# Two layers of a hybrid encoder: GLA values loaded a group earlier, other shares of dense work, the decays moved, the convolutions' gate product on another engine

## The chip, the cores and the metric

The kernel runs on one core of a Trainium2 chip. The metric is the device time of one execution in microseconds (us), the median of the runs shown. The engines of the core work side by side, each through its own list of instructions in order: TensorE (PE, with its weight loads as PEld), VectorE (DVE), ScalarE (ACT), GpSimd (POOL) and SyncE (SP), which here issues the transfers between the core's memory and the chip's main memory.

## What is computed

Two layers, each with one input projection whose columns feed three mixers: gated linear attention (GLA), a gated delta rule with short convolutions, and cross-attention into 256 memory tokens. Sequence 1024, model width 1024, all in f32.

```python
def _layer(x, mem, ...):
    h = _rmsnorm(x, norm_w)
    proj = jnp.einsum('btd,de->bte', h, w_in)
    (gla_q, gla_k, gla_v, gla_z, gla_lr, gdn_qkv, gdn_z, gdn_b, gdn_a, xa_q, xa_z) = _split_cols(proj, IN_SIZES)
    ...
    o1 = _run_bidir(_gla_chunked, (q1, k1, v1, log_alpha_fwd), (q1, k1, v1, log_alpha_bwd))
    o1 = _rmsnorm(o1, gla_norm_w) * silu(gla_z)
    qkv = jax.nn.silu(_centred_depthwise_conv(gdn_qkv, gdn_conv_w))      # 5 taps
    q2, k2, v2 = _split_cols(qkv, ...)
    q2 = _l2norm(q2) * (GDN_DK ** -0.5)
    k2 = _l2norm(k2)
    ...
    o2 = _run_bidir(_gated_delta_chunked, (q2, k2, v2, g_fwd, beta_fwd), (q2, k2, v2, g_bwd, beta_bwd))
    o2 = _rmsnorm(o2, gdn_norm_w) * silu(gdn_z)
    o3 = softmax-attention of xa_q into the memory tokens, normed, * silu(xa_z)
    return x + concat(o1, o2, o3) @ w_out

def _gla_chunked(q, k, v, g):       # per chunk: cumulated gates, a state update from k and v, then
    ...                             # S_t = dec * S_{t-1} + st
def _gated_delta_chunked(q, k, v, g, beta):
    diff = gc[..., :, None] - gc[..., None, :]
    decay = jnp.where(incl, jnp.exp(jnp.where(incl, diff, 0.0)), 0.0)
    ...
```

## The kernel before

**Dense work.** The input projection is cut into tiles of 128 columns by 1024 tokens. `dense_gen` is a generator that walks over them; one step of it is a unit of six matmuls (weights and activations are split into a high and a low half, Hh and Hl against wh and wl). `pull` takes units worth a number of nanoseconds, `upto` takes them until a tile is done. The other phases run beside this generator and pull units between their own steps, so that TensorE has something to do. At a tile's second half `conv_sink` or `spill` takes it on.

**Convolutions (`conv_sink`, `phase_proj`).** Nine tiles feed the convolutions, k first, then v, then q. ScalarE copies a tile out of PSUM into `pad` and, scaled by the middle tap, into `acc`. VectorE adds the four other taps (four `scalar_tensor_tensor`, L537). ScalarE forms the sigmoid in three passes (`pad`), and the product `acc * pad` ends the SiLU. TensorE transposes it to token order (`conv_t`), k and q are normed (`l2norm`) and transposed back (`back_t`).

**Decays (`decays`).** For each of four heads: a subtract on POOL (N minus gB, pinned in its place), a minimum with a cap on VectorE, an exponential on ScalarE. One `next(dec)` emits one head. The kernel before emits heads in the k loop and, what is left, in the v loop.

**The chain (`phase_mix`, `chain`).** The gated delta rule goes through 16 steps of both directions, one chunk each; `chain_load` brings kq, row, kv and qkt for a step. Between the pieces of a step `filler` emits other work by a time budget: the GLA gates and states, then dense units, then the mixing tiles (`mixes`: memory attention xa and GLA output), then the output projection.

**GLA (`gla_pre`).** Eight groups (a pair of heads, a direction, a half of the sequence). `gate` loads q and k, forms the gates and stores the scaled pair ge_d; `state` loads the values gv, transposes, and forms the states, which it stores (s_d). Gates run two groups ahead of states. gv has one buffer before. The order of the work is that of the code, with a scheduler that reorders within each engine; all loads and stores stand in SyncE's one queue.

**Constants that spread the dense units.** `DEN0` units after the second piece of the GLA work, `PRE_D` units spread over its 24 pieces, `MIX0` units between the last state and the first mixing tile, `MIXN` the pace after that. `DC0` is the index of the k loop from which decays are emitted.

## Time and profile before

| what | value |
| --- | --- |
| median of 3 runs | 1389.29 us (1388.51 to 1390.2) |
| the profiled execution | 1388.65 us, span 1386.9 us |
| PE busy | 1214.1 us (88% of the span) |
| DVE, ACT, POOL busy | 827.7, 614.0, 462.4 us |
| chain that ended last | PE 48%, DVE 15%, DMA 14%, POOL 6%, SPq 6%, ACT 6%, issue 5% |
| PE idle before mm matmuls | 22.2 us, of it 17.5 until the accumulator on ACT |
| POOL products acc*pad | 18 instructions, 45.5 us |

How to read it: the span is the time between the first and the last instruction of the profiled execution. Busy time is the sum of an engine's instructions; weight loads (PEld) overlap the matmuls. Work that a wait holds up stands in brackets behind an instruction, with the idle time before it and the name of what ended it. Lines such as L537 are lines of the kernel before; the new kernel's lines are one or two lower in the first half of the file. A row's "x8" is a count of instructions.

### The profile page before, as it was taken

The numbers are of one execution on the slowest core, as the hardware profiler recorded it, in microseconds if no ns is written. First come the engines' busy times: TensorE is split into PE (matmuls) and PEld (weight loads), VectorE is DVE, ScalarE is ACT, GpSimd is POOL, SyncE is SP. The second block draws the span as 40 slices with busy tenths as digits, with TensorE's granted clock in tenths as the row PEclk, the third lists the DMA queues.
The fourth block names the chain that finished last, engine by engine and source line by source line (L and its number), as shares of the span: only waits on it lengthen the run. The fifth ranks groups of instructions, "written<-read, shape, count | busy, mean of one in ns | idle before, by whom it ended". The sixth has DMA issues, their size and how long they took to land.

```text
span 1386.9 us, 25327 instructions
## 1 busy us (share of the span) xinstructions
PE 1214.1 (88%) x9962; PEld 991.1 (71%) x9962; DVE 827.7 (60%) x1255; ACT 614.0 (44%) x1293; POOL 462.4 (33%) x493
## 2 busy tenths in 40 slices
PE   6998799998888647999989987999977887589997
PEld 6986588776666546787879866887756666468886
DVE  5336855795376655655373568647944786465553
ACT  5334655343556432233163356543345565232432
POOL 4026442294335231211230444423943443220111
PEclk9999999999999868999999998999999898699999
DMA  7151234532999895345471513345228999853532
GB/s 230 57 129 46 86 112 130 190 99 70 206 234 240 252 243 116 92 134 154 155 226 48 135 31 118 88 133 186 91 86 220 241 250 251 220 158 95 160 104 107
DMA packets 299319, 205.38 MB, mean 148 GB/s; under 512 B 144064, under 2 KB 267392, under 8 KB 299200
## 3 DMA queue, kind: packets, MB, share of 16 engines
q1 hardware_dynamic: 297040, 195.89, 51.5%
q10 hardware_dynamic: 2016, 7.34, 1.6%
q8 instruction: 79, 1.29, 0.4%
q0 software_dynamic: 144, 0.52, 0.1%
q14 instruction: 40, 0.33, 0.1%
HBM read 145.11 MB, written 58.59 MB: 147 GB/s over the span
## 4 chain that ended last, share of the span: by engine, by line
PE 48%; DVE 15%; DMA 14%; POOL 6%; SPq 6%; ACT 6%; issue 5%; DVEq 0%; ACTq 0%; POOLq 0%
PE mm L98 31%; DVE acc L537 6%; PE cp L98 4%; PE x L98 3%; PE tr L101 3%; DMA gv<-vg 3%; PE R L98 2%; POOL X L90 2%; DMA wor<-in_w_out_dram 2%; POOL tmp L90 2%; PE gb L98 1%; DMA ge_d<-qe 1%; ACT pad L84 1%; DMA wr<-in_w_in_dram 1%; POOL sp L90 1%
## 5 line engine op out<-in xcount | busy, mean ns | idle before, releaser
L98 PE MATMUL mm<-Hh,wh 128*128 128x512 f32 x736 | 311.1, 423 | 22.2 <-ACT acc L84 17.5
L98 PE MATMUL mm<-Hl,wh 128*128 128x512 f32 x736 | 295.9, 402 | 0.0
L98 PE MATMUL mm<-Hh,wl 128*128 128x512 f32 x736 | 295.5, 402 | 0.0
L90 POOL TENSOR_TENSOR wl<-wr,wh 128x1024 fp32r<-128x1024 f32 x46 | 119.4, 2596 | 277.0 <-ACT wh L84 250.3
L98 PEld LDWEIGHTS mm<-Hh,wh 128*128 128x128 f32 x736 | 143.3, 195 | 59.8 <-ACT acc L84 20.9
L537 DVE SCALAR_TENSOR_TENSOR acc<-pad,convw,acc 128x1024 f32<-128x1024 f32 x72 | 141.4, 1963 | 67.5 <-ACT acc L84 53.1
L98 PE MATMUL mm<-wo,oh 128*128 128x512 f32 x512 | 166.7, 407 | 0.3 <-DVE xr L87 0.3
L98 PEld LDWEIGHTS mm<-Hh,wl 128*128 128x128 f32 x736 | 143.2, 195 | 32.3
L98 PEld LDWEIGHTS mm<-Hl,wh 128*128 128x128 f32 x736 | 144.1, 196 | 26.2
L90 POOL TENSOR_TENSOR ol<-z,oh 128x512 fp32r<-128x512 f32 x32 | 41.0, 1286 | 197.9 <-ACT oh L84 196.8
L98 PEld LDWEIGHTS mm<-wo,oh 128*128 128x128 f32 x512 | 90.5, 189 | 18.6 <-issue 0.9
L98 PE MATMUL mm<-wo,ol 128*128 128x512 f32 x256 | 101.2, 395 | 0.0
L90 POOL TENSOR_TENSOR acc<-acc,pad 128x1024 f32<-128x1024 f32 x18 | 45.5, 2528 | 109.8 <-ACT pad L84 109.8
L84 ACT ACTIVATE wh<-wr 128x1024 fp32r<-128x1024 f32 x46 | 48.5, 1054 | 68.6 <-PE mm L98 57.6
L90 POOL TENSOR_TENSOR kq<-kq,row 96x512 f32<-96x512 f32 x30 | 41.8, 1395 | 101.6 <-DMA kq<-kq_d 45.7
L90 POOL TENSOR_TENSOR S<-S,dec 96x384 f32<-96x384 f32 x56 | 53.3, 967 | 62.5 <-DVE S L87 53.8
L90 POOL TENSOR_TENSOR sp<-sp,sg 128x512 f32<-128x512 f32 x32 | 45.9, 1434 | 59.7 <-ACT sg L84 41.8
L84 ACT ACTIVATE oh<-z 128x512 fp32r<-128x512 f32 x32 | 20.2, 632 | 85.0 <-DVE z L87 84.9
L98 PE MATMUL cp<-S,kq 96*64 96x96 f32 x960 | 51.7, 256 | 7.0 <-DVE oa L87 2.4
L98 PEld LDWEIGHTS mm<-wo,ol 128*128 128x128 f32 x256 | 48.1, 188 | 11.5
L98 PEld LDWEIGHTS cp<-S,kq 96*64 96x64 f32 x960 | 44.2, 141 | 16.0 <-issue 7.0
L87 DVE TENSOR_TENSOR xr<-mm,xr 128x512 f32<-128x512 f32 x32 | 22.1, 690 | 50.7 <-PE mm L98 24.7
(294 smaller groups left out, 2439.5 us busy)
## 6 DMA issues: line engine op xcount, KB each, us to landing
wr<-in_w_in_dram SPq DMA_DIRECT2D x46, 512.0 KB, 3.9
kq<-kq_d SPq DMA_DIRECT2D x64, 192.0 KB, 4.5
kv<-kv_d SPq DMA_DIRECT2D x64, 192.0 KB, 4.4
zT<-sp SPq DMA_DIRECT2D x32, 256.0 KB, 3.4
ge_d<-qe SPq DMA_DIRECT2D x32, 256.0 KB, 4.4
wor<-in_w_out_dram SPq DMA_DIRECT2D x16, 512.0 KB, 5.4
z<-zT SPq DMA_DIRECT2D x16, 512.0 KB, 4.4
gqk<-ge_d SPq DMA_DIRECT2D x16, 512.0 KB, 4.2
```

What stands on the lines that cost most here:

```text
L84: return self.nc.scalar.activation(out, in_, func, **kw)
L87: return self.nc.vector.tensor_tensor(out, a, b, op=op)
L90: return self.nc.gpsimd.tensor_tensor(out, a, b, op=op)
L98: return self.pin(self.nc.tensor.matmul(*args, **kw))
L101: return self.pin(self.nc.tensor.transpose(*args, **kw))
L537: nc.vector.scalar_tensor_tensor(acc, pad[:, j:j + T], self.convw[:, f, j:j + 1], acc, op0=ALU.mult, op1=ALU.add)
```

## The change

The new kernel has four edits. (1) The product that ends a convolution's SiLU is on VectorE (`tt`) where it was on POOL (`ptt`): 18 instructions. (2) The decays' heads are emitted in the q loop, from its second convolution on, the rest before q's norm; the `next(dec)` of the k and v loops and `DC0` are gone. (3) The load of a GLA group's values is in a function of its own, `values`, called once ahead of everything and then one group before its state; the values have two buffers. (4) `PRE_D` 32 to 24, `MIX0` 5 to 8, `DEN0` 6 to 4.

```diff
-PRE_D = 32
+PRE_D = 24
-DC0 = 0
-MIX0 = 5
+MIX0 = 8
-DEN0 = 6
+DEN0 = 4
...
                 self.sigmoid(pad[:, 0:T], acc)
-                self.ptt(acc, acc, pad[:, 0:T], ALU.mult)
+                self.tt(acc, acc, pad[:, 0:T], ALU.mult)
                 self.conv_out[f] = acc
...
             self.conv_t(3 + i, k_tok[:, :, i * 128:i * 128 + 128])
-            if i >= DC0:
-                next(dec, None)
         self.l2norm(ST, k_tok, 1.0)
...
             v_out(1 + i)
-            next(dec, None)
...
             self.conv_t(i, q_tok[:, :, i * 128:i * 128 + 128])
+            if i:
+                next(dec, None)
         for _ in dec:
             pass
         self.l2norm(ST, q_tok, HD ** -0.5)
...
+        def values(pr, d, hf):
+            v = G.tile([P, 4, 2, HD], F32, tag="gv", name="gv", bufs=2)
+            nc.sync.dma_start(v.rearrange("p t a b -> p t (a b)"),
+                              self.vg[hf * 4:hf * 4 + 4, :, pr * 192:pr * 192 + 192].rearrange("t p c -> p t c"))
+            st["v"] = st.get("v", []) + [v]
+
         def state(pr, d, hf):
...
-            v = G.tile([P, 4, 2, HD], F32, tag="gv", name="gv", bufs=1)
-            nc.sync.dma_start(v.rearrange("p t a b -> p t (a b)"),
-                              self.vg[hf * 4:hf * 4 + 4, :, pr * 192:pr * 192 + 192].rearrange("t p c -> p t c"))
+            v = st["v"].pop(0)
...
+        values(*groups[0])
         for g in groups[0:2]:
             gate(*g)
             yield
         for i, g in enumerate(groups):
             if i + 2 < len(groups):
                 gate(*groups[i + 2])
                 yield
+            if i + 1 < len(groups):
+                values(*groups[i + 1])
             for _ in state(*g):
                 yield
             yield
```

What this does to the order of instructions, in layer 0. First SyncE, in the middle of the GLA groups. ge_d is the store of a gate's result, qkin the loads of a gate's q and k, gv the values, s_d the store of a state; kq, row, kv and qkt belong to the chain, wor is a raw piece of the output weights. The kernel before:

```order
L1174 DMA ge_d<-qe 64x2x512 x2
L1142 DMA qkin<-qg 128x512
L1143 DMA qkin<-kg 128x512
L993 DMA kq<-kq_d 96x8x64 x2
L1192 DMA gv<-vg 128x4x192
L995 DMA row<-row_d 96x4x64 x2
L1425 DMA wor<-in_w_out_dram 128x2x512
L1222 DMA s_d<-sb 64x4x96 x2
L997 DMA kv<-kv_d 64x2x384
L998 DMA qkt<-qkd 64x4x64
```

The same place in the new kernel:

```order
L1172 DMA ge_d<-qe 64x2x512 x2
L1140 DMA qkin<-qg 128x512
L1141 DMA qkin<-kg 128x512
L993 DMA row<-row_d 96x4x64
L991 DMA kq<-kq_d 96x8x64
L1186 DMA gv<-vg 128x4x192
L991 DMA kq<-kq_d 96x8x64
L993 DMA row<-row_d 96x4x64
L1224 DMA s_d<-sb 64x4x96 x2
L995 DMA kv<-kv_d 64x2x384 x2
L996 DMA qkt<-qkd 64x4x64 x2
```

The place of gv in the list is alike, but before it brings the values of the state that s_d stores a few rows below, and now those of the next group's state.

Next VectorE at the first convolutions. acc is a convolution's accumulator, tok the k values in token order, N the decays, cap their cap. The kernel before:

```order
L537 SCALAR_TENSOR_TENSOR acc<-pad,convw,acc 128x1024 x8
L87 TENSOR_TENSOR N<-N,cap 128x1024
L115 COPY tok<-tr 128x4x128
L537 SCALAR_TENSOR_TENSOR acc<-pad,convw,acc 128x1024 x4
L87 TENSOR_TENSOR N<-N,cap 128x1024
```

The new kernel:

```order
L536 SCALAR_TENSOR_TENSOR acc<-pad,convw,acc 128x1024 x4
L86 TENSOR_TENSOR acc<-acc,pad 128x1024
L536 SCALAR_TENSOR_TENSOR acc<-pad,convw,acc 128x1024 x4
L114 COPY tok<-tr 128x4x128
L86 TENSOR_TENSOR acc<-acc,pad 128x1024
```

A product of accumulator and sigmoid stands behind each four multiply-adds, where the minimums of the decays stood behind some.

Last VectorE at q's norm, where tok holds the q values, ssq the sums of squares, and qT the q values transposed back. The kernel before:

```order
L115 COPY tok<-tr 128x4x128 x2
L561 TENSOR_REDUCE ssq<-sq 128x8 x2
L87 TENSOR_TENSOR tok<-tok,ssq 128x768 x2
L561 TENSOR_REDUCE ssq<-sq 128x8 x2
L87 TENSOR_TENSOR tok<-tok,ssq 128x768 x2
L115 COPY qT<-tr 96x512 x4
```

The new kernel:

```order
L86 TENSOR_TENSOR N<-N,cap 128x1024
L114 COPY tok<-tr 128x4x128
L560 TENSOR_REDUCE ssq<-sq 128x8
L86 TENSOR_TENSOR N<-N,cap 128x1024
L560 TENSOR_REDUCE ssq<-sq 128x8
L86 TENSOR_TENSOR N<-N,cap 128x1024
L86 TENSOR_TENSOR tok<-tok,ssq 128x768
L560 TENSOR_REDUCE ssq<-sq 128x8
L86 TENSOR_TENSOR tok<-tok,ssq 128x768 x2
L560 TENSOR_REDUCE ssq<-sq 128x8
L86 TENSOR_TENSOR tok<-tok,ssq 128x768
L114 COPY qT<-tr 96x512 x4
```

Three of the four minimums now stand between the last copy of a convolution and the norm's last product; on POOL the last three subtracts stand one right behind the other there.

On TensorE the order of the dense units against the chain differs too: both kernels have 35 units between the first gate matmul and the first mixing matmul of a layer; before, the last group's state matmuls stand in chain step 9 with none of these units behind them, and now in step 7 with 8 units behind them. The mixing starts with step 10 before and with step 9 now.

## Rows read from the trace of the kernel before

**Rows 1.** Stretches: start:end, length, busy (x count) PE PEld DVE ACT POOL, PEclk, DMA, GB/s.

```profile
85.00:172.70 87.70, 73.95 (x328) 59.51 (x327) 65.17 (x41) 46.14 (x68) 41.28 (x25) 0.96 0.31 79
172.70:241.00 68.30, 68.30 (x341) 56.84 (x339) 37.52 (x33) 36.67 (x56) 22.52 (x13) 0.98 0.42 120
359.00:499.25 140.25, 107.39 (x1130) 83.29 (x1128) 90.58 (x184) 75.33 (x157) 53.54 (x45) 0.90 1.01 241
775.00:862.50 87.50, 74.75 (x326) 59.83 (x325) 66.25 (x41) 46.16 (x68) 42.37 (x25) 0.94 0.29 78
1049.30:1187.35 138.05, 111.61 (x1130) 86.56 (x1129) 97.19 (x185) 74.93 (x157) 52.02 (x45) 0.88 0.91 245
```

**Rows 2.** SyncE's queue, timeline: start, length, what; gates' and mixing's first loads.

```profile
359.01 0.60 SPq L1125 DMA_DIRECT2D gb<-in_gla_b_dram  x1
...
499.25 1.13 SPq L1347 DMA_DIRECT2D kraw<-mkv  x2
...
1049.30 1.14 SPq L1125 DMA_DIRECT2D gb<-in_gla_b_dram  x1
...
1187.35 1.11 SPq L1347 DMA_DIRECT2D kraw<-mkv  x2
```

**Rows 3.** The tile gv: what its users sat idle for (us, times).

```profile
  DMA gv<-vg: 28.1, 8
```

**Rows 4.** TensorE's timeline: start, length, what, [idle before <- what ended it].

```profile
477.39 0.91 PE L98 MATMUL x<-gv,kt 128*64 128x96 f32 x8 [8.99 <-DMA gv<-vg]
...
508.15 0.55 PE L98 MATMUL x<-kh,xq 128*128 128x256 f32 x1 [8.75 <-DMA xq<-xq]
...
1194.32 0.55 PE L98 MATMUL x<-kh,xq 128*128 128x256 f32 x1 [8.78 <-DMA xq<-xq]
```

**Rows 5.** The chain of waits in the convolutions: start, length, what.

```profile
115.27 3.36 DVE acc L537
...
118.65 2.85 DVE acc L537
...
121.53 1.30 DVE acc L537
```

**Rows 6.** POOL's timeline at the same place.

```profile
112.82 2.36 POOL L90 TENSOR_TENSOR acc<-acc,pad 128x1024 f32<-128x1024 f32 x1 [3.38 <-ACT pad L84]
115.14 2.39 POOL L90 TENSOR_TENSOR wl<-wr,wh 128x1024 fp32r<-128x1024 f32 x1
...
117.57 2.84 POOL L90 TENSOR_TENSOR N<-N,gB 128x1024 f32<-128x1024 f32 x1
```

**Rows 7.** TensorE's timeline at the same place.

```profile
115.29 0.50 PE L98 MATMUL mm<-Hh,wh 128*128 128x512 f32 x1 [1.55 <-ACT acc L84]
```

**Rows 8.** VectorE's groups, 85 to 172.7 us: what, count, busy, mean ns, idle before.

```profile
L537 DVE SCALAR_TENSOR_TENSOR acc<-pad,convw,acc 128x1024 f32<-128x1024 f32 x24 | 49.2, 2051 | 27.0 <-ACT acc L84 14.7 <-DMA N<-gcr_d 11.7
...
L87 DVE TENSOR_TENSOR N<-N,cap 128x1024 f32<-128x1024 f32 x4 | 4.9, 1218 | 1.8 <-POOL N L90 1.8
```

**Rows 9.** POOL's groups in the same stretch.

```profile
L90 POOL TENSOR_TENSOR wl<-wr,wh 128x1024 fp32r<-128x1024 f32 x6 | 16.6, 2772 | 28.8 <-ACT wh L84 21.0 <-DVE ssq L561 7.8
L90 POOL TENSOR_TENSOR acc<-acc,pad 128x1024 f32<-128x1024 f32 x5 | 13.2, 2637 | 21.1 <-ACT pad L84 21.1
L90 POOL TENSOR_TENSOR N<-N,gB 128x1024 f32<-128x1024 f32 x4 | 11.3, 2813 | 0.0
```

**Rows 10.** ScalarE's timeline: an exponential of the decays.

```profile
110.74 1.06 ACT L84 ACTIVATE N<-N 128x1024 f32<-128x1024 f32 x1 [0.75 <-DVE N L87]
```

**Rows 11.** VectorE's timeline at the end of the query norm.

```profile
228.41 3.26 DVE L87 TENSOR_TENSOR tok<-tok,ssq 128x768 f32<-128x768 f32 x2
```

**Rows 12.** TensorE's timeline at the same place.

```profile
231.88 1.03 PE L101 MATMUL tr<-ident,tok 128*96 128x128 f32 x8
```

**Rows 13.** TensorE's timeline in the chain: two groups of one step.

```profile
419.14 0.88 PE L98 MATMUL cp<-vn,qkt 64*64 64x96 f32 x16
...
423.13 1.54 PE L98 MATMUL cp<-S,kq 96*64 96x96 f32 x32
```

## The prediction

> **What bounds the kernel now.** I read the busy time of each engine in stretches first, because the page's 88% for TensorE is an average over stages with different limits. The profiled execution took 1388.65 us, 0.64 us under the median of the runs (1389.29); its span is 1386.9 us. The reader should compare TensorE's busy time with the length of each stretch [rows 1]. In the stretch of the k and v convolutions it does 73.95 us in 87.70 (13.75 idle; in layer 1 74.75 in 87.50, 12.75 idle). In the query convolutions it has no idle time at all, 68.30 in 68.30. From the first load of the GLA gates to the first load of the mixing it does 107.39 in 140.25 and, in layer 1, 111.61 in 138.05 (32.9 and 26.4 idle). So an edit can save time in the first and third stretch of each layer, and lose it in the second.
>
> What holds the third stretch? I read SyncE's queue next. Between the gates' first load and the mixing's first load it issues in order [rows 2] 174 loads and stores in layer 0 and 173 in layer 1 (counted in the order of the kernel), so 140.24 / 174 = 0.806 us for each and 138.05 / 173 = 0.798; the transfer engines are busy for a share of 1.01 and 0.91 of that time [rows 1]. The waits agree: TensorE stands idle 28.1 us, eight times, for the GLA values gv [rows 3], 8.99 us of it at the worst one, and then 8.75 and 8.78 us for the first query of the mixing [rows 4]. This stretch goes at the pace of SyncE and its transfers, not at that of arithmetic.
>
> What holds the first stretch? There I read the chain of waits: the first three of a convolution's four multiply-adds on VectorE take 3.36, 2.85 and 1.30 us though they are alike [rows 5]. The two long ones stand beside POOL's gate product and its subtract for the decays [rows 6]: POOL's product runs from 112.82 to 115.18, its weight remainder to 117.5, and the subtract from 117.57 to 120.41, and the third multiply-add, with POOL idle, costs 1.30. TensorE then stands idle 1.55 us for the accumulator that ScalarE evacuates late [rows 7].
>
> **The convolutions' product on VectorE.** Over the stretch the 24 multiply-adds cost 49.2 us, 2.05 each [rows 8]; at 1.30 they would take 31.2, so 18.0 us of VectorE is blocking. Of POOL's work beside them (wl 16.6, products 13.2, decays' subtracts 11.3, together 41.1 [rows 9]) the products and the subtracts leave this stretch: 24.5 of 41.1, or 60%. If blocking goes with POOL's time, 10.7 us of it goes. The decays' four minimums (4.9 us [rows 8]) leave VectorE too, and five products come, priced by the minimum of the same shape at 1.23 us: 6.2. VectorE does 10.7 + 4.9 - 6.2 = 9.4 us less, and ScalarE's four exponentials (1.06 us [rows 10], 4.2 together) leave the same queue that evacuates TensorE. TensorE has 13.75 and 12.75 us of idle time to give, so I take 9 per layer, 18 in all. The bounds: all idle time goes, 26.5; or wl alone keeps the whole blocking, and the gain is 4.9 - 6.2 = -1.3 per layer, a loss of 2.6. I take 9 since it is the row for a free VectorE (1.30) that I have twice. A new wait comes with it: the product stands in VectorE's order behind the sigmoid on ScalarE, and the next convolution's multiply-adds and the copies of the transposes stand behind the product. Those multiply-adds wait for an evacuation that ScalarE does after that same sigmoid, so this costs nothing while TensorE's next tile is not done sooner; where it is, the bound above holds it.
>
> Weighed against a rule: the two long multiply-adds are blocked for about as long as POOL's instruction lasts (3.36 and 2.85 against 1.30). The Trainium skill, "SBUF — State Buffer", section "Who interferes with whom", says that a VectorE instruction with two SBUF inputs and a GpSimd instruction that reads SBUF exclude each other and that the later one is fully blocked; the trace agrees. By that rule the edit in the next part is dearer than I take it (the third rival).
>
> **The decays beside the queries.** All of their work moves from a stretch where TensorE idles to one where it doesn't: four subtracts on POOL (11.3 us per layer), four minimums (4.9), four exponentials (4.2). It issues no transfer. Cover: TensorE's dense units. The query norm has little: VectorE ends it at 228.41 + 3.26 = 231.67 [rows 11] and TensorE reads it at 231.88 [rows 12], 0.21 us later. In the new order three of the four minimums stand among the norm's reductions and products, 3 x 1.23 = 3.7 us; one more blocked instruction costs 2.85 - 1.30 = 1.55. So 3.7 + 1.55 - 0.21 = 5 us per layer, 10 in all. Bounds: 0, if TensorE has a dense unit to do in that time, and 4 x (2.81 + 1.22 + 1.06) = 20.4 per layer, if each head's three steps stand one behind the other. I take 5 because the minimums are in the order and the back-to-back subtracts begin before them.
>
> **Values a group ahead, dense work spread anew.** The values' load is issued one group earlier, into a second buffer, so it no longer stands behind the loads of the chain. The dense units: the order has 35 of them in both kernels between the first gate and the first mixing matmul, but in the new one 8 stand behind the last state matmul, none before. So the GLA groups are done sooner, in chain step 7 and not 9, and the mixing starts with step 9 and not 10. Between the gates' first load and the mixing's first load SyncE issues 154 transfers in both layers: 20 fewer and 19 fewer. They aren't gone; they stand behind, where the transfer engines are no longer full. At the prices above this is 20 x 0.806 = 16.1 and 19 x 0.798 = 15.2 us. Against it stands one chain step, which now runs after the mixing's start, and whose TensorE work is 1.54 for its outputs and three groups of some 0.88, 4.2 us [rows 13]. The gain: 16.1 - 4.2 = 11.9 and 15.2 - 4.2 = 11.0, 22.9 in all. Bounds: 0, where the queue takes as long for what it carries first, and 28.1 + 8.75 + 8.78 - 2 x 4.2 = 37.2, where every wait for the values and the first query goes. The second buffer and the earlier issue cost no engine anything: the same eight loads per layer. A tile more of the mixing now shares PSUM with the chain; I price it at nothing, since the chain's step waits for SyncE there, and at one step (4.2) if that cover is gone.
>
> **The sum.** 22.9 + 18 - 10 = 30.9; 1388.65 - 30.9 = 1357.8, and with the 0.64 us to the median, 1358.
>
> **The rivals.** *The transfers are the bound* and the stretch takes its 140 us whatever is issued first: the share of 1.01 in layer 0 speaks for it, the 0.91 in layer 1 and the waits for single loads against it. Then 1388.65 - 18 + 10 = 1380.7, 1381 with the difference to the median.
>
> *VectorE's order is the bound* (slower than before). From the first k convolution to the query transposes is 87.70 + 68.30 = 156 us. If the products wait for the sigmoid and the multiply-adds gain nothing, and the decays stand one behind the other before the norm's end (20.4), the stretch grows by 20.4 per layer against the gain of 11.5 in the third: 1388.65 + 2 x (20.4 - 11.5) = 1406.5, so 1407. It decides from 156 + 11.5 = 167.5 us. Against it: VectorE is busy 65.17 us of 87.70 and 37.52 of 68.30.
>
> *The query norm pays for POOL in full.* Three subtracts of 2.81 us run back to back on POOL and each holds an instruction of the norm whole: 8.4 + 3.7 = 12.1 per layer, 24.2 in all instead of 10. 1388.65 - 22.9 - 18 + 24.2 = 1372, 1373 with the difference. That the norm is a chain with 0.21 us to spare speaks for it; that the subtracts begin earlier, beside the last convolutions, against it. The rule cited above is the mechanism.
>
> *Nothing is moved that counts*: the waits for gv turn into waits for the chain's kq, row and kv, and what the convolutions gain the queries lose (9 against 9): about 1389, no change.
>
> *More goes*: every wait for the values and the first query (37.2) and all the idle time of the convolutions (26.5), less the 10: 1388.65 - 53.7 = 1335, 1336 with the difference.
>
> **How the numbers follow.** The forecast 0.48; the transfers' bound 0.16; the query norm in full 0.13; more 0.05; VectorE's order 0.12; nothing 0.06. Faster by over 0.2% (2.8 us, about what a measurement of this kernel can tell from no change) is 0.48 + 0.16 + 0.13 + 0.05 = 0.82; the same 0.06; slower 0.12. The range leaves out the last two, 0.18: from 1333 (more) to 1382 (the transfers' bound), and the forecast's own terms, between 8 and 37 for the third stretch, lie within it.
>
> **What would show it.** In the new profile: multiply-adds of the convolutions near 1.3 to 1.6 us each, not 2.05, and a TensorE idle time of 5 us, not 13.75, in that stretch; the values' waits gone, and the first load of the mixing some 124 us after the gates' first, not 140.25; the queries' stretch 68 + 5 us. It is wrong if the multiply-adds stay at 2 us, if the time from gates to mixing stays at 138 to 140 us though 20 fewer transfers are in it, or if the query stretch grows by over 12.

## The result, and the profile after

The changed kernel takes 1373.13 us (median of 3 runs, 1367.09 to 1374.81) against 1389.29: a ratio of 0.9879, with a 95% interval of 0.9849 to 0.9908. It is faster by 16 us where 31 were forecast. A second set of four runs gave 1368.2 against 1391.4 (0.9837, 0.9816 to 0.9857): 23 us. Which of these is nearer the mark the runs don't settle; both fall short of the 31. The profiled execution, with 1367.09 us and a span of 1365.2, is the fastest of the first three, so the trace accounts for 21.7 us of span.

The stretches of the new profile, beside [rows 1]: start:end, length, then busy time (x instructions) of PE, PEld, DVE, ACT and POOL, the granted clock, the DMA share and GB/s. They are chosen by the work in them, so their bounds have moved: k and v convolutions, queries, and gates to mixing in layers 0 and 1. The granted clock is 1.00 at the upper of TensorE's two levels (2.4 GHz) and 0.50 at the lower (1.2 GHz); in between it is a mean over the stretch.

```profile
85.00:163.00 78.00, 72.01 (x333) 59.11 (x332) 56.03 (x43) 45.34 (x66) 15.26 (x16) 0.98 0.40 101
163.00:237.00 74.00, 69.00 (x337) 56.97 (x335) 47.25 (x39) 38.27 (x57) 22.17 (x13) 0.95 0.35 99
354.40:478.70 124.30, 96.68 (x962) 75.02 (x963) 76.48 (x161) 65.93 (x142) 41.47 (x38) 0.88 0.96 236
1034.20:1154.60 120.40, 96.89 (x975) 74.55 (x975) 78.70 (x161) 67.33 (x144) 40.26 (x39) 0.90 0.91 243
```

The convolutions' stretch has 6 us of TensorE idle where it had 13.75, the queries' stretch 5.0 where it had none, and the time from the gates' first load to the mixing's is 124.3 and 120.4 us where it was 140.25 and 138.05.

VectorE's groups from 85 to 163 us, beside [rows 8] (busy us, mean ns, idle before), show why the convolutions gained:

```profile
L536 DVE SCALAR_TENSOR_TENSOR acc<-pad,convw,acc 128x1024 f32<-128x1024 f32 x24 | 37.6, 1570 | 15.5 <-ACT acc L83 14.7
L86 DVE TENSOR_TENSOR acc<-acc,pad 128x1024 f32<-128x1024 f32 x5 | 6.1, 1224 | 12.3 <-ACT pad L83 12.3
```

A multiply-add takes 1.57 us on average, not 2.05, and the product its 1.22. VectorE waits 12.3 us for the sigmoid, which is the new wait. It costs TensorE little: its transposes wait 2.8 us for the product on VectorE in this stretch, where they waited 1.6 for the one on POOL, and its matmuls wait 2.5 us for the accumulator on ScalarE, not 8.7.

Behind the average stand two kinds of multiply-add. 19 of the 24 take 1.27 to 1.29 us, and the other five begin while POOL's weight remainder wl is running. One of them, the first of the four at 112.64:

```profile
111.56 2.39 POOL L89 TENSOR_TENSOR wl<-wr,wh 128x1024 fp32r<-128x1024 f32 x1
112.64 6.42 DVE L536 SCALAR_TENSOR_TENSOR acc<-pad,convw,acc 128x1024 f32<-128x1024 f32 x4 [1.34 <-ACT acc L83]
```

It ends at 115.03, 1.08 us after wl (113.95). In the kernel before 12 of the 24 are lengthened, and each of them ends 1.1 us after the POOL instruction that began ahead of it.

From the first convolution's transposes to the first of the query norm (k, v and query convolutions together), layers 0 and 1, before:

```profile
105.88:231.88 126.00, 112.25 (x520) 91.49 (x519) 86.75 (x62) 70.12 (x104) 57.31 (x36) 0.96 0.30 85
795.36:921.65 126.29, 113.54 (x520) 92.17 (x518) 87.79 (x62) 69.97 (x104) 55.56 (x33) 0.95 0.30 85
```

After:

```profile
105.96:220.10 114.14, 108.15 (x520) 89.48 (x519) 80.72 (x66) 69.16 (x99) 30.27 (x25) 0.99 0.32 90
787.45:899.79 112.34, 108.33 (x519) 89.32 (x518) 80.56 (x66) 68.99 (x99) 30.32 (x25) 0.98 0.32 92
```

TensorE's idle time falls by 7.8 and 8.7 us, and the same matmuls take 4.1 and 5.2 us less, at a granted clock that is higher by 0.03.

TensorE's timeline at the query norm, beside [rows 12]: the first transposes come 11.8 us sooner, but where the kernel before did the first eight in one go, the new one is held up three times by VectorE, and the last group of eight starts 14.64 us after the first, not 6.76 (238.64 - 231.88 before).

```profile
220.10 0.38 PE L100 MATMUL tr<-ident,tok 128*96 128x128 f32 x2
223.00 0.42 PE L100 MATMUL tr<-ident,tok 128*96 128x128 f32 x2 [2.53 <-DVE tok L86]
223.96 0.40 PE L100 MATMUL tr<-ident,tok 128*96 128x128 f32 x2 [0.54 <-DVE tok L86]
226.30 0.66 PE L100 MATMUL tr<-ident,tok 128*96 128x128 f32 x2 [1.94 <-DVE tok L86]
...
234.74 1.03 PE L100 MATMUL tr<-ident,tok 128*96 128x128 f32 x8
```

The three waits are 5.0 us of the 7.9 by which this part is longer. The rest is the clock. The same part, from the first to the last of these transposes, before and after, and the six us around the last wait:

```profile
231.88:239.41 7.53, 7.53 (x51) 6.59 (x50) 2.06 (x3) 2.39 (x5) 0.00 (x0) 1.00 0.68 211
220.10:235.50 15.40, 10.40 (x50) 8.24 (x49) 7.55 (x8) 4.22 (x11) 2.03 (x1) 0.78 0.44 128
224.00:230.00 6.00, 4.06 (x14) 3.06 (x15) 2.32 (x3) 0.57 (x3) 0.00 (x0) 0.53 0.60 182
```

The same matmuls take 2.9 us longer, at a granted clock of 0.78 where it was 1.00: behind the first two waits it falls to the lower level, and it is back at 1.00 from 232 us on. In layer 1 the waits are 4.7 us and the same matmuls again take 2.9 longer.

VectorE is late there because of the minimums, which stand ahead of the norm's copy and among its instructions. POOL's three subtracts, one minimum and the norm's first product:

```profile
209.25 6.72 POOL L89 TENSOR_TENSOR N<-N,gB 128x1024 f32<-128x1024 f32 x3
211.22 2.94 DVE L86 TENSOR_TENSOR N<-N,cap 128x1024 f32<-128x1024 f32 x1 [4.18 <-POOL N L89]
218.97 0.94 DVE L86 TENSOR_TENSOR tok<-tok,ssq 128x768 f32<-128x768 f32 x1
```

The minimum waits for the first subtract and is then held up by the second (2.94 us, where a free one takes 1.21); the last copy of query values stands behind it. The subtracts end at 215.97, before any product of the norm.

And what TensorE waits for between the gates and the mixing in layer 0 (us in total, times, longest), where [rows 3] and [rows 4] showed the values and the first query:

```profile
PE R L97 <- DVE ve L86: 9.1, 6, 2.9
PE x L100 <- ACT ge L83: 7.2, 1, 7.2
PE x L97 <- DVE U L1220: 5.3, 1, 5.3
PE x L97 <- ACT ge L83: 3.1, 2, 2.5
```

No wait for the values is left in either layer (28.1 us before), and the wait for the first query went from 8.75 us to 0.7 (in a second profile of the changed kernel it is 3.8, and 2.2 in layer 1). But TensorE still idles 27.6 us in the stretch (124.30 - 96.68), 32.9 before. In their stead it waits for the gates' exponentials and the states U, and longer for the chain's ve (9.1 us, 5.6 before).

The decisive view goes from the gates' first load to the start of the state matmuls of the chain's last step, which is called the chain's end from here on. Before, layers 0 and 1, then the rest behind the chain's end in layer 1:

```profile
359.00:577.70 218.70, 166.01 (x1908) 132.32 (x1908) 133.10 (x274) 97.37 (x222) 70.45 (x63) 0.87 0.85 206
1049.30:1260.30 211.00, 165.36 (x1910) 131.63 (x1911) 138.05 (x274) 96.97 (x222) 67.89 (x62) 0.88 0.80 215
1260.30:1386.90 126.60, 119.45 (x874) 95.66 (x870) 64.29 (x117) 45.23 (x122) 18.07 (x14) 0.99 0.38 123
```

After, the same three stretches:

```profile
354.40:575.70 221.30, 175.38 (x1936) 139.86 (x1935) 132.63 (x276) 98.09 (x224) 67.46 (x64) 0.88 0.85 207
1034.20:1245.00 210.80, 172.27 (x1938) 135.94 (x1937) 134.28 (x276) 98.80 (x224) 65.36 (x63) 0.89 0.82 220
1245.00:1365.20 120.20, 113.31 (x843) 90.97 (x842) 62.84 (x115) 44.12 (x120) 16.80 (x13) 0.98 0.38 122
```

The mixing begins 16 and 18 us sooner, and the chain's end doesn't: 221.3 and 210.8 us, where it took 218.7 and 211.0. What changed is that 28 more matmuls are done before that end (1936 against 1908), and 31 fewer behind it, which takes 120.2 us instead of 126.6. TensorE's idle time before the chain's end went from 52.7 to 45.9 us and from 45.6 to 38.5, and its busy time there grew by 9.4 and 6.9. What remains behind the chain's end is 5.9 us shorter in layer 0 (up to the next layer's first convolution) and 6.4 in layer 1. With the chain's end 2.6 us later in layer 0 and 0.2 sooner in layer 1, this part gains 3.3 and 6.6 us.

From the mixing's first load to the chain's end, layers 0 and 1 before, then after:

```profile
499.25:577.70 78.45, 58.63 (x782) 49.04 (x780) 42.52 (x91) 22.04 (x65) 16.91 (x19) 0.80 0.58 141
1187.35:1260.30 72.95, 53.76 (x780) 45.07 (x782) 40.85 (x90) 22.04 (x65) 15.87 (x18) 0.87 0.59 159
478.70:575.70 97.00, 78.70 (x980) 64.84 (x974) 56.15 (x115) 32.16 (x83) 25.99 (x26) 0.88 0.71 171
1154.60:1245.00 90.40, 75.38 (x964) 61.40 (x963) 55.59 (x115) 31.47 (x81) 25.09 (x25) 0.89 0.70 189
```

TensorE does 20.1 and 21.6 us more in it. Two groups of layer 0 show what that is, the chain's outputs (16 matmuls a step) and the output projection, before and then after:

```profile
L98 PE MATMUL cp<-vn,qkt 64*64 64x96 f32 x80 | 4.8, 263 | 0.0
L98 PE MATMUL mm<-wo,oh 128*128 128x512 f32 x12 | 4.1, 421 | 0.0
L97 PE MATMUL cp<-vn,qkt 64*64 64x96 f32 x112 | 7.5, 284 | 0.0
L97 PE MATMUL mm<-wo,oh 128*128 128x512 f32 x28 | 10.2, 448 | 0.0
```

Two more steps of the chain lie in it (about 9 us of TensorE), more of the output projection (42 of its matmuls, 18 before, 7 us) and three dense units (4.6 us; two in layer 1). The mixing's own matmuls ahead of the chain's end are nearly as many as before (396, 392). The code says why: each piece of a chain step takes other work of the same nominal amount from `filler` (`FILL`, `FILL2`, `FILLW` and `FILL3` are all 1950), so an earlier mixing only brings later work ahead of the chain's end in TensorE's list. It cannot shorten that list, only the idle time in it.

### The profile page after: what moved, and what is told of

It reads as the page before. It is cut to its first block, busy times and chain, and to the rows that moved or that the text cites. A ratio compares the mean times of both kernels' runs of the same rounds, so it can differ in the third digit from the quotient of the medians.

```text
span 1365.2 us, 25327 instructions
## 1 busy us (share of the span) xinstructions
PE 1212.5 (89%) x9962; PEld 989.6 (72%) x9962; DVE 820.5 (60%) x1273; ACT 615.8 (45%) x1293; POOL 401.2 (29%) x475
## 3 DMA queue, kind: packets, MB, share of 16 engines
q8 instruction: 79, 1.29, 0.4%
## 5 line engine op out<-in xcount | busy, mean ns | idle before, releaser
L97 PE MATMUL mm<-Hh,wh 128*128 128x512 f32 x736 | 307.5, 418 | 11.4 <-ACT sg L83 6.0
L89 POOL TENSOR_TENSOR wl<-wr,wh 128x1024 fp32r<-128x1024 f32 x46 | 112.6, 2447 | 319.2 <-ACT wh L83 307.9
L97 PEld LDWEIGHTS mm<-Hl,wh 128*128 128x128 f32 x736 | 142.2, 193 | 25.8
L536 DVE SCALAR_TENSOR_TENSOR acc<-pad,convw,acc 128x1024 f32<-128x1024 f32 x72 | 116.0, 1614 | 36.3 <-ACT acc L83 33.8
L89 POOL TENSOR_TENSOR S<-S,dec 96x384 f32<-96x384 f32 x56 | 50.2, 912 | 78.8 <-DVE S L86 76.6
L83 ACT ACTIVATE oh<-z 128x512 fp32r<-128x512 f32 x32 | 20.1, 632 | 90.0 <-DVE z L86 88.7
L97 PE MATMUL cp<-S,kq 96*64 96x96 f32 x960 | 52.7, 268 | 0.4 <-POOL S L89 0.4
L86 DVE TENSOR_TENSOR ve<-R,end 128x384 f32<-128x384 f32 x32 | 17.7, 552 | 57.2 <-ACT vn L83 57.2
```

The costliest lines, as they stand in the source:

```text
L83: return self.nc.scalar.activation(out, in_, func, **kw)
L86: return self.nc.vector.tensor_tensor(out, a, b, op=op)
L89: return self.nc.gpsimd.tensor_tensor(out, a, b, op=op)
L97: return self.pin(self.nc.tensor.matmul(*args, **kw))
L536: nc.vector.scalar_tensor_tensor(acc, pad[:, j:j + T], self.convw[:, f, j:j + 1], acc, op0=ALU.mult, op1=ALU.add)
```

## Experiments

Times are medians; ratios are against the kernel before on the same chip. One profiled execution stands behind each reading of a stretch. The second set of the changed kernel (1368.2 us) is from the same chip as the run of the values with the shares, the run of the product alone and the one of product and decays. All other runs are from other chips, so their distance to 1368.2 is less sure, and by the first set's 1373.1 it is 5 us less.

**The whole change again.** No edit.

> The changed kernel once more, for a closer time to set the parts against. Its three runs spread from 1367 to 1375 us; both theories expect 1370 to 1373, 16 to 19 us under the kernel before.

Measured: 1368.2 us (4 runs, 1367.8 to 1372.6) against 1391.4: 0.9837 (0.9816 to 0.9857), a little under the 1370 to 1373 expected. This is the base for the runs below, and its trace (chain's end 221.5 and 211.3 us behind the gates) is the one that their traces are set against.

**The values and the dense shares alone.** The two edits of the GLA groups; product and decays as before.

```diff
-PRE_D = 32
+PRE_D = 24
...
-MIX0 = 5
+MIX0 = 8
...
-DEN0 = 6
+DEN0 = 4
...
+        values(*groups[0])
...
+            if i + 1 < len(groups):
+                values(*groups[i + 1])
```

> Of the change only the values a group ahead and the new shares of dense work; the product stays on POOL and the decays beside k and v. Theory A (the chain of 16 steps ends no sooner, so only the TensorE idle time that goes before its end counts: 52.7 to 45.9 us in layer 0 and 45.6 to 38.5 in layer 1 of the changed kernel's trace): 12 to 14 us gain, about 1376. Rival B (the earlier mixing is worth the forecast 22.9 us, and something else in the full change takes it back): about 1366.

Measured: 1385.4 us (12 runs, 1377.2 to 1391.1), a ratio of 0.9955 (0.9936 to 0.9975): a gain of 6 us. Rival B is out. Theory A is right in kind, but its 12 to 14 us were too much. The profiled run (span 1387.9) shows the mixing's first load 122.2 and 120.5 us behind the gates' first, 18 sooner than before, and the chain's end no sooner: 221.1 and 218.3 us behind the gates, against 218.7 and 211.0. The stretch to the chain's end in layer 1, in this run:

```profile
1048.01:1266.34 218.33, 178.11 (x1929) 141.56 (x1925) 134.16 (x276) 99.32 (x224) 65.57 (x62) 0.84 0.79 211
```

Its idle time is 40.2 us, nearly as short as the changed kernel's 38.5. But its matmuls take 178.1 us where the changed kernel's take 172.3, at a granted clock of 0.84 against 0.89. In layer 1 this is one reason why the run falls short of Theory A.

**The values alone, and the dense shares alone.** First the values, with the two buffers:

```diff
+        values(*groups[0])
...
+            if i + 1 < len(groups):
+                values(*groups[i + 1])
```

> Of the change only the values a group ahead, with two buffers; the shares of dense work as before. TensorE's 28 us of waits for the values should go. Theory A (the chain's end sets the time, and it comes no sooner): no change within 4 us, 1387 to 1393, and the mixing's first load 5 us sooner at the most. Rival B (those waits were on the path): a gain of 12 to 20 us, 1371 to 1379.

Measured: 1395.4 us (12 runs), 1.0043 (1.0023 to 1.0062): slower by 6. The time from gates to mixing stays (143.9 us, 139.6 in layer 1). What TensorE waits for, from the gates to the chain's end, layer 0:

```profile
PE x L98 <- DMA xq<-xq: 18.9, 1, 18.9
PE x L98 <- DVE U L1222: 9.3, 3, 6.9
PE R L98 <- DVE ve L87: 6.3, 4, 4.4
```

Rival B is out, and Theory A's 1387 to 1393 is just missed. The wait for the values is gone and that for the first query has grown from 8.75 to 18.9 us. SyncE's list up to the mixing is no shorter (177 transfers, 174 before). TensorE, rid of the first wait, is at the first query 135.6 us behind the gates, not 140.4, and the load lands later.

Then the shares:

```diff
-PRE_D = 32
+PRE_D = 24
...
-MIX0 = 5
+MIX0 = 8
...
-DEN0 = 6
+DEN0 = 4
```

> Of the change only the new shares of dense work; the values are loaded as before. Theory A: fewer dense units ahead of the last state, so the mixing starts sooner, by about 10 us, and TensorE has somewhat less left after the chain's end: 3 to 6 us gain, 1385 to 1388. Rival B: without the early values the GLA groups wait for them as before, and nothing is gained: 1389 to 1393.

Measured: 1393.9 us (12 runs), 1.0046 (1.0026 to 1.0066): slower by 4.4, just beyond what Rival B allowed. The same view, layer 0:

```profile
PE x L98 <- DMA gv<-vg: 13.1, 4, 6.9
PE x L101 <- ACT pe L84: 8.4, 4, 6.8
PE x L101 <- ACT ge L84: 7.5, 1, 7.5
```

The mixing comes sooner (123.4 and 120.3 us behind the gates, so the dense shares do this, not the values), the chain's end comes later (223.4 and 226.3 us), and behind it 120.3 us are left, as in the full change. Each edit alone costs time, together they gain 6 us. The waits fit this account: the shares move the mixing up and cover its first load (no wait for the first query in this run), and only the early values keep the GLA groups from waiting while there is less dense work beside them. How much of the 6 and the 4.4 us is instead the order that the scheduler gives the other engines (see below) no run shows.

**The cover of the mixing's first loads.**

```diff
-MIX0 = 8
+MIX0 = 0
```

> The changed kernel with none of the 8 dense units between the last state and the first mixing tile (MIX0 = 0); the order ahead of that place is the changed kernel's. By the forecast's step (an earlier mixing brings the end nearer one for one, less the step that then runs behind it) the mixing's first load comes some 10 us sooner and the time falls by 6 us per layer: 1354 to 1360. Theory A (the units cover the mixing's first loads, and the chain's end comes no sooner): the wait for the first query comes back, some 9 us in each layer, the chain's end does not move forward, and the time is 1368 to 1380.

Measured: 1393.7 us (12 runs), 1.0034 (1.0017 to 1.005): 25 us slower than the changed kernel's second set and 20 slower than its first. TensorE's timeline at the mixing's first matmul in layer 0:

```profile
486.38 0.55 PE L97 MATMUL x<-kh,xq 128*128 128x256 f32 x1 [19.42 <-DMA xq<-xq]
```

In layer 1 the wait is 17.5 us. The mixing's first load is issued 121.3 us behind the gates, 3 sooner than in the full change, so less dense work in front brings it hardly nearer: SyncE's list is what it waits for (148 transfers at 0.82 us). The chain's end comes 9.2 and 17.4 us later than in the changed kernel (230.7 and 228.8 against 221.5 and 211.3), with 12.6 and 16.8 us more of TensorE idle time. The forecast's "one for one" is out. The loss is above Theory A's 1368 to 1380, which took the returning wait at 9 us, not at 19.

**The chain by itself.** All other work waits until its 16 steps are done.

```diff
-            ns += self.budget
+            ns += 0
...
-        self.alias = {}
+        self.alias = {"gx": "ga", "x": "ga"}
```

> The changed kernel with no other work between the chain's steps: the GLA groups, the dense units, the mixing and the output all come after it. A measurement of the chain by itself, not a better kernel. If the chain's own latency and its own loads set its pace (13 us a step, 16 steps): 200 to 220 us for it still. If it is the work between its steps that sets the pace: 110 to 150 us. The whole becomes much longer, 1480 to 1600 us.

Measured: 1537.4 us (one run). The stretch of the chain, layer 0, where no other work is left in TensorE's list:

```profile
361.00:505.00 144.00, 103.90 (x1160) 88.03 (x1160) 45.24 (x116) 14.64 (x30) 41.72 (x44) 0.57 0.66 118
```

144 us, some 9 us a step, though the granted clock is 0.57 here (near the lower of the two levels) and was 0.88. So the chain's own latency is not what makes its end come after 220 us; the work between its steps, in TensorE's one list, and the waits of that work are. The expectation's first alternative falls.

**The product alone, and with the decays.**

```diff
-                self.ptt(acc, acc, pad[:, 0:T], ALU.mult)
+                self.tt(acc, acc, pad[:, 0:T], ALU.mult)
```

> Of the change only the product on VectorE; the decays stay beside the k and v convolutions. If blocking goes with POOL's time, the products' 13.2 us of 41.1 free 5.8 us per layer and put 6.2 on VectorE: about no change, 1387 to 1391. If VectorE's longer multiply-adds were held by the product above all: 6 to 10 us per layer, 1370 to 1377.

Measured: 1382.7 us (6 runs), 0.9940 (0.9917 to 0.9963): a gain of 8.7, between the two alternatives. VectorE's multiply-adds from 85 to 172.7 us, in that run:

```profile
L537 DVE SCALAR_TENSOR_TENSOR acc<-pad,convw,acc 128x1024 f32<-128x1024 f32 x24 | 42.9, 1789 | 19.1 <-DMA N<-gcr_d 11.7 <-ACT acc L84 7.0
```

With the decays moved as well:

```diff
-            if i >= DC0:
-                next(dec, None)
...
-            next(dec, None)
...
+            if i:
+                next(dec, None)
```

> Of the change the product on VectorE and the decays beside the queries, values and dense work as before. The changed kernel's trace shows the convolutions 11.8 and 13.9 us shorter and the query norm some 7 longer in each layer: theory A, 25.7 - 14 = 12 us gain, about 1377. Rival B: if the missing gain is lost in this part, 0 to 5 us gain, 1384 to 1389.

Measured: 1381.6 us (6 runs), 0.9922 (0.9904 to 0.9939): a gain of 9.8. Theory A expected 12. Its multiply-adds in the same stretch:

```profile
L537 DVE SCALAR_TENSOR_TENSOR acc<-pad,convw,acc 128x1024 f32<-128x1024 f32 x25 | 38.0, 1523 | 17.9 <-DMA N<-gcr_d 12.1 <-ACT acc L84 5.0
```

The product's leaving takes 0.26 us off the 2.05 and the decays' another 0.27, about in proportion to POOL's time, as the forecast had assumed (6.2 and 6.4 us over 24 multiply-adds, against 5.8 and 4.9 by its rule). One by one it is a count: 12 of 24 multiply-adds are held up before, 9 of 24 without the products, 5 of 25 without the subtracts too. But the decays' move brings 1 us in the whole: the query norm pays it back (7.5 us before, 15.4 in this run).

**The decays earlier, out of the norm.** Two heads behind each of the first two query convolutions.

```diff
-            if i:
-                next(dec, None)
+            next(dec, None)
+            next(dec, None)
```

> The changed kernel with the decays earlier: two heads after each of the first two query convolutions, so that no minimum stands in the query norm. If the norm's 7 us per layer in the changed kernel come from the minimums and POOL's subtracts in it (theory C): the last query transposes come some 7 us sooner in each layer, 1354 to 1360. If the norm is slow for another reason, or the time is only moved behind the query stretch: 1365 to 1370, as the changed kernel.

Measured: 1385.9 us (12 runs, 1381.4 to 1394.2), 0.9984 (0.9960 to 1.0008): 18 slower than the changed kernel's second set, 13 than its first. The norm is rid of its waits (its last transposes now come some 20 us behind the last convolution's, not 26, at a granted clock of 1.00), but the convolutions wait for the products instead. What TensorE waits for from 85 to 245 us:

```profile
PE tr L100 <- DVE acc L86: 8.0, 3, 3.5
PE mm L97 <- ACT acc L83: 2.6, 2, 1.9
```

The minimums now stand among the multiply-adds, ahead of the products. Neither alternative had this. From the first convolution's transposes to the norm's end this makes 0.6 us in layer 0 and 4.3 in layer 1. Half of the 18 us lies elsewhere: the chain's stretch is 220.3 us in layer 1, not 211.3, in a place that the edit doesn't touch. TensorE's list is the same there; those of SyncE, ScalarE, VectorE and POOL hold the same instructions in another order (in layer 1, 183 of SyncE's 223 transfers keep their order), which the scheduler gives them.

**Work that nobody reads, to move that order alone.** Transposes of the identity ahead of the GLA gates, with a copy of each four of them; first 16 per layer, then 4.

```diff
+        tiny = R.tile([P, 4, 128], F32, name="tiny")
+        for _ in range(4):
+            ps = self.tr()
+            for j in range(4):
+                self.tpose(ps[:, j, :], self.ident, self.ident)
+            nc.vector.tensor_copy(tiny, ps)
         self.gla_gate_ops(l, GQ, R)
```

> The changed kernel with sixteen transposes of the identity and four copies of their result, which nobody reads, ahead of the GLA gates in each layer: some 2.5 us of TensorE per layer, 5 in all. They make the scheduler order SyncE, ScalarE and VectorE in the chain's stretch anew (in SyncE's list 195 of 783 rows move), and there the order becomes that of the run with the decays early. Theory S (the order that the scheduler gives the chain's stretch is worth some 10 us by itself): 1378 to 1388, with layer 1's chain some 8 us longer. Rival (the order there costs nothing, and the decays' run lost its time to the decays): 1371 to 1375, that is the changed kernel and the 5 us.

Measured: 1409.9 us (6 runs), 1.0139 (1.0112 to 1.0166), above both ranges. The 16 cost far more where they stand than I had expected: the time from the query norm to the gates grows by 9.7 and 8.3 us, of which TensorE waits some 4 for the copies and works some 5. The chain's stretch is 229.9 and 219.5 us against 221.5 and 211.3. In layer 1 that is the length of the run with the decays early (220.3), which has nearly the same order there; in layer 0 it is not (221.9). So this run is only half an answer.

> The same with four transposes and one copy per layer: 0.6 us of TensorE per layer, 1.3 in all; 104 of SyncE's 783 rows move. Theory S: anything from 1362 to 1385, but not 1369 within 2 us. Rival: 1369 to 1371.

Measured: 1377.9 us (6 runs, 1376.3 to 1378.6), 0.9912 (0.9889 to 0.9935), against 1368.2 for the changed kernel in its second set. That is 9.7 us for some 1.3 us of work; by the first set's 1373.1 it is 4.8, and the intervals of the two ratios then overlap. The chain's stretch in layer 1, where TensorE's list is the changed kernel's, beside 210.80 with 172.27 busy above:

```profile
1035.40:1254.70 219.30, 173.12 (x1937) 138.43 (x1935) 133.23 (x276) 98.90 (x224) 65.15 (x63) 0.87 0.79 211
```

It does the same work (1937 matmuls, 173 us busy) in 8.5 us more, 7.7 of it idle time. In layer 0 it is 3.2 us shorter than in the changed kernel, and 3.5 us of the difference lie between the query norm and the gates, where the transposes stand. So a reordering that no line of the change asks for moves a stretch by as much as the parts of the change do, and it can go either way. The changed kernel has, in layer 1, the shortest chain's stretch of all runs with the new shares (211 us; the others 214.5 to 228.8); in layer 0 it hasn't (221.3 and 221.5; the others 216.3 to 230.7).

**The decays put back in the full change.**

```diff
+            if i >= DC0:
+                next(dec, None)
...
+            next(dec, None)
...
-            if i:
-                next(dec, None)
```

> The changed kernel with the decays back beside the k and v convolutions. The run with the product alone had its multiply-adds at 1.77 us, with the decays moved too at 1.49, and the query norm then 5 us slower: theory (the decays' move is worth about nothing by itself, -1 us in the runs without the new shares): 1367 to 1372, or by theory S some 8 us beside it for the order of the chain's stretch. Rival (the move is worth what the sum of the parts lacks, 7 us): 1374 to 1378.

Measured: 1377.6 us (6 runs, 1376.8 to 1379.6), 0.9912 (0.9891 to 0.9933): 9.4 slower than the whole change in its second set, 4.5 in its first. Both alternatives allow this. In the trace the stretch from the first convolution to the norm's end is 2.2 and 4.5 us longer without the move, and the chain's is 5.2 shorter in layer 0 and 3.2 longer in layer 1. The move is worth 1 us beside the product alone and 4.5 to 9 beside everything; the runs don't separate its own worth from that of the order it sets off.

## Why the prediction was right or wrong

**Direction and range held, the size didn't.** The range, 1333 to 1382, holds the time; 31 us were forecast and 16 came in the first set of runs, 23 in the second. That the sum lies no further off is in part luck. The forecast had no term for the granted clock, which brought 9.3 us in the convolutions and took 5.8 in the norm; the 3.5 us left of that made up for some of the 13 us that the step about the mixing lacked. By the stages of the profiled execution (21.7 us):

**The product on VectorE (forecast 18).** More than forecast: from the first convolution's transposes to the first of q's norm, layer 0 went from 126.0 to 114.1 us (11.9) and layer 1 from 126.3 to 112.3 (13.9), 25.8 in all. This counts decays and product together, as the forecast's 9 per layer did. Of it 16.5 are TensorE's idle time, which is what the forecast had counted, so its mechanism and its size are right: multiply-adds at 1.57 us, idle time 6 us. The other 9.3 us are the same matmuls at a higher granted clock, with fewer waits between them; the forecast had no term for that. The allocation of the blocking by POOL's time held on average (2.05 to 1.79 to 1.52). One reading was wrong: the two long multiply-adds of [rows 5] do not stand beside the gate product, which ends at 115.18, before the first of them begins (115.27), but beside the weight remainder and the subtract of [rows 6], and each ends 1.1 us after these. The price of the new wait was small (TensorE waits 2.8 us for the product, 1.6 before). The wl remainder stays and keeps the average above 1.30.

**The decays beside the queries (forecast 10 of loss).** Mis-sized: the norm's transposes take 7.9 and 7.6 us longer, 15.5 in all, against 5 per layer. The waits are the forecast's (VectorE's minimums in the norm, no slack): 5.0 and 4.7 us. What the sum lacked is what came behind them, 2.9 us per layer of the same matmuls at a granted clock of 0.78, where it had been 1.00. The rival of the query norm paying for POOL in full (12.1 per layer) did not come about: the three subtracts are done at 215.97, three us before the norm's first product, and what they hold up are two minimums, by 1.7 and 0.3 us, and no reduction or product of the norm. That rival went by the full blocking of which the Trainium skill tells ("SBUF — State Buffer", section "Who interferes with whom"). The trace agrees with the rule, one instruction at a time: the minimum at 211.22 began beside a subtract that ends at 213.09, and lasted until 214.17. What the rival had wrong is which instructions stand side by side. The experiment with the decays earlier shows that the place was not badly chosen: out of the norm they hold the products.

**Values and dense shares (forecast 22.9).** This is the step that failed. Its first half was exact: 154 transfers at 0.806 us are 124.1 us from the gates to the mixing, and 124.3 were measured (122.9 and 120.4 in layer 1); the wait for the values (28.1 us) went to 0 and that for the first query (17.5) to 0.7, or 6.0 in the second profile. The step that takes these 16.1 and 15.2 us for time saved, less one chain step of 4.2 us, was wrong. From the mixing's first load to the chain's end it now takes 97.0 us, not 78.45, and in layer 1 90.4 (1245.0 - 1154.6), not 72.95. What moved behind the mixing's first load is not 4.2 us of TensorE but 20.1 and 21.6: two steps of the chain, dense units, and work of the output projection that had stood behind the chain's end, since the chain's pieces take the same amount of other work whatever it is. With somewhat less idle time beside it that is 17 to 19 us, about as much as was saved. The gain that there is came another way, through TensorE's idle time before the chain's end, 6.8 and 7.1 us less. In the profiled execution that is 3.3 us in layer 0 (the chain's end 2.6 later, 5.9 less behind it) and 6.6 in layer 1 (0.2 sooner, 6.4 less), so 9.9 against 22.9; 25.8 - 15.5 + 9.9 are 20.2 of the 21.7, and some 1.5 us lie between the query norm and the gates.

**Whether the parts add up.** The product and decays alone gain 9.8 us, the values and shares alone 6.0; together 23.2 in the same set. By the first set's 16 us nothing would be missing, so the 7 us rest on the second. The 4-transpose run shows that the order that the scheduler gives SyncE, ScalarE, VectorE and POOL in the chain's stretch shifts with a small edit upstream and moved that stretch by some 8 us in one layer and by 3 the other way in the other. That this explains the missing 7 us is argued, not shown: no run holds that order fixed while a part of the change is taken out. The clock is a rival that no run separates from it: in the run with values and shares alone a lower one went with 5.8 us of longer matmuls in layer 1. No version was faster than the changed kernel.

**The rivals.** The transfers' bound (1381) described the run with the values alone rather than the change: time to the mixing unchanged, the wait moved. VectorE's order as the bound, slower than before, did not happen; what there is of it, the 5 us of waits at the norm in each layer and the 8.0 us of the run with the early decays, is of its kind. For *more goes* the prediction gives 1336 and lets its range begin at 1333; nothing hangs on the difference.

## What to carry to other kernels

When a wait is removed in a stretch where one engine's list holds several streams, the price of what moves behind must be counted as all the work that the list then puts ahead of the last stream's end (here 20 us of TensorE), not as one stream's step (4.2): look at where the last of the streams ends, how much work the program places before that, and at the idle time in it. An early load and the work that covers its successor can each cost time alone and gain together, so test the pair. Count a wait of TensorE with the matmuls behind it: here 5 us of waits brought 3 us of slower matmuls with them. And where a scheduler orders the engines, let a dummy edit show first how much the order itself is worth; below that, a comparison of single parts tells little.

## What the runs showed of the hardware

POOL holds up VectorE's instructions one by one, and in proportion only on average. A multiply-add takes 1.27 to 1.29 us, or, where it began while POOL's product, subtract or weight remainder was running, ends 1.1 us after that instruction. The average of 2.05 us fell to 1.79 when five products left POOL and to 1.52 when four subtracts left too.

The granted clock followed TensorE's waits: 1.00 in the query norm without waits and 0.78 with 5 us of them, with the same matmuls 2.9 us longer. It bears on the comparison of whole runs too. In layer 1's stretch from the gates to the chain's end it was 0.89 in the changed kernel, 0.87 in the run with four transposes, and 0.84 to 0.86 in the runs with the values, the shares or both alone and in the one without the cover, so part of what sets these apart is the clock. Without other work between the steps it was granted at 0.57.
